# Convolution states of a hybrid encoder layer: one transfer and copies on chip in place of one small transfer for each tile

## The chip, the core and the metric

The kernel runs on one core of a Trainium2 chip. The metric is the device time of one execution in microseconds (us). The engines are TensorE (PE; PEld is its weight load), VectorE (DVE), ScalarE (ACT), GpSimd (POOL) and SyncE (SP), which issues every DMA of this kernel on one queue (SPq in the rows).

## The reference

One step of a one-layer encoder over T = 1152 columns: 1024 of a prompt, then 8 samples of 16. Cut to what matters here:

```
h  = rmsnorm(x);  split(h @ w_in)                # mixer A: sparse attention, mixer B: gated delta rule
ext = concat([conv_b_buf, conv_in])              # 3 old values per channel and sequence, 1536 channels
new_conv_b = ext[:, T:]                          # the last 3 go out as the new state
cb  = silu(causal_dwconv(ext, conv_b))           # width 4, then the delta rule
x   = x + (sigmoid(ga) * ya + sigmoid(gbr) * yb) @ w_out
ext_f = concat([ffn_buf, u_gate])                # 2 old values per channel and sequence, 2816 channels
new_ffn = ext_f[:, T:]
x   = x + (gelu(causal_dwconv(ext_f, conv_ffn)) * u_val) @ w_down
```

The prompt starts from a state of zeros; the 8 samples bring one each (`state_gdn_conv`, `state_ffn_conv`). Both kinds of new state are outputs.

## The kernel before, in words

Channels lie on partitions, time on columns. Products are made of two fp32r parts each (H and L of the activations, wh and wl of the weights), three matmuls for a tile of 128 channels by 384 columns (`acc`), later 288 (`up`) and 384 (`dn`). A small driver in the kernel (`_Driver`) runs many generators as threads against an own clock of costs and writes every engine's instructions in the order that comes out; `yield SP` asks for a place in the DMA queue, `yield self.exts` for a buffer, `yield DMA` or an event for a landing. `pick` gives an element-wise operation to the one of two engines that is free first on that clock. So an edit at one place changes the order of what comes after it on all engines.

The stages, by the time of the profile: normalisation and first products (0 to 120 us); the input projection, with the indexer (`ix`, its queries `qr` loaded from DRAM), the width-4 convolutions of 12 channel tiles, the selection of keys and the local part of the delta rule (`gd`) beside it (120 to 650); attention, the scan of the delta rule and the samples (`at`) with dense products as filler (650 to 1060); the output projection; the `up` products of 22 channel tiles with the width-3 convolution (1205 to 1710); the `down` products (to 2075); the end.

The two places of the change:

- `evac_conv`: an evacuated tile goes into an extended buffer `ext` (two of them, `exts`). In block 2 (last 256 prompt columns and the samples) the view `es` holds 8 rows of 3 + 16 columns. The 3 state columns come by a DMA from `in_sc_b`, 128 partitions by 8 runs of 12 bytes; the last 3 columns of the prompt and of each sample go out by two DMAs to `out_cb`, and `ext` is given back behind them.
- `evac_up` and `up_inner`: the same for the up-projection with a buffer `fe` (two), states of 2 columns: a DMA from `in_sc_f` (8 runs of 8 bytes for each partition), two DMAs to `out_cf`, then `AT[f]` is stored, and `load_up` reads it back (`xs<-AT`) for the down products.

Of the kernel before, what the change touches and what calls it, by code (L numbers as in the profile page):

```python
# [7 lines left out]
F32 = mybir.dt.float32  # L8
# [12 lines left out]
TP = 1024  # L21
# [9 lines left out]
PE, ACT, DVE, POOL, SP, DMA = "pe", "act", "dve", "pool", "sp", "dma"  # L31
# [269 lines left out]
class _Kernel:  # L301
# [382 lines left out]
    def mixers(self):  # L684
        I, drv = self.I, self.drv
# [12 lines left out]
        self.cvp = conv.enter_context(self.tc.tile_pool(name="cv", bufs=1, side="right", reuse_waits="tile"))  # L698
        self.exts = _Banks(self.cvp, [128, 412], "ext", 2)
        self.cvs = _Banks(self.cvp, [128, BW], "cvc", 2)  # L700
        first = [None, 4, 5, 8, 9, 10]
        order = [(f, (0,)) for f in first] + [(None, (1, 2))] + [(f, (0, 1)) for f in range(4)]
        rest = [*range(16, 28), 4, 28, 5, 29, 6, 30, 7, 31, *range(8, 16), *range(32, 48)]
# [61 lines left out]
    def first_loads(self, jobs, p):  # L765

        nc, I, drv = self.nc, self.I, self.drv
# [34 lines left out]
        yield DVE  # L802
        nc.vector.tensor_scalar(self.cwb, self.cwb, 0.5, None, op0=OP.mult)
        nc.vector.tensor_scalar(self.ngd, self.ngd, 0.5, None, op0=OP.mult)

    def arrival(self, ev, t):
        self.drv.cur.dma = t
# [152 lines left out]
    def evac_conv(self, f):  # L960

        nc, O, I = self.nc, self.O, self.I
        h, kind = divmod(f - 16, 4)
        ch = (kind - 1) * 4 + h
        last = self.cvp.tile([128, 2, 3], F32, name="last", bufs=4)

        def go(b, cols, acc):
            w = self.cwb[:, ch]
            ext = yield self.exts
            es = ext[:, 259:411].rearrange("p (b q) -> p b q", q=19)  # L970
            n = BW if b < 2 else 256
            if b < 2:
                yield from self.scaled(ext[:, 3:3 + n], acc, b)
                yield POOL
                nc.gpsimd.tensor_copy(last[:, b], ext[:, BW:BW + 3])
            else:
                yield ACT
                nc.scalar.copy(ext[:, 3:3 + n], acc[:, :n])
                nc.scalar.copy(es[:, :, 3:], acc[:, 256:].rearrange("p (b q) -> p b q", q=16))
                self.drv.give(self.accs, acc)  # L980
            yield POOL
            if b == 0:
                nc.gpsimd.memset(ext[:, 0:3], 0.0)
            else:
                nc.gpsimd.tensor_copy(ext[:, 0:3], last[:, b - 1])
            if b == 2:
                yield SP
                nc.sync.dma_start(es[:, :, 0:3], I["sc_b"][ch])
                yield DMA
            c = yield self.cvs  # L990
            t = yield self.evs
            groups = [(c[:, :n], [ext[:, j:j + n] for j in range(4)])]
# [2 lines left out]
            for o, src in groups:  # L995
                yield ACT
                nc.scalar.activation(o, src[0], AF.Copy, scale=w[:, 0:1])
                for j in range(1, 4):
                    if j == 2:
                        u = t[:, :n] if len(o.shape) == 2 else t[:, 256:].rearrange("p (b q) -> p b q", q=16)  # L1000
                        yield ACT
                        nc.scalar.activation(u, src[j], AF.Copy, scale=w[:, j:j + 1])
                        yield POOL
                        nc.gpsimd.tensor_add(o, o, u)
                    else:
                        yield DVE
                        nc.vector.scalar_tensor_tensor(o, src[j], w[:, j:j + 1], o, op0=OP.mult, op1=OP.add)
            if b == 2:
                yield SP
                nc.sync.dma_start(O["cb"][ch][:, 0:3], ext[:, 256:259])  # L1010
                nc.sync.dma_start(O["cb"][ch][:, 3:27].rearrange("p (b q) -> p b q", q=3), es[:, :, 16:19])
            self.drv.give(self.exts, ext)
            yield ACT
            nc.scalar.activation(t, c, AF.Tanh)
            yield DVE
# [1547 lines left out]
    def evac_out(self, d):  # L2563
# [61 lines left out]
            drv.give(self.xs, x)  # L2625
        return go

    def up_parts(self, t):

        nc = self.nc  # L2630
# [35 lines left out]
    def evac_up(self, j, bank):  # L2666

        nc, drv, p, f = self.nc, self.drv, self.fp, j.f
# [20 lines left out]
        drv.give(self.ups, bank[A1X])  # L2689
        ext = yield self.exts  # L2690
        es = ext[:, 1026:].rearrange("p (b q) -> p b q", q=18)
        yield SP
        nc.sync.dma_start(es[:, :, 0:2], self.I["sc_f"][f])
        yield POOL
        nc.gpsimd.memset(ext[:, 0:2], 0.0)
        g, R = parts(ext[:, 2:2 + T]), parts(self.R2)
        if f == 0:

# [13 lines left out]
            x = own(u1)  # L2712
        else:
# [12 lines left out]
            x = own(u2)  # L2726
# [10 lines left out]
    def up_inner(self, j, ext, v):  # L2737

        nc, drv, f = self.nc, self.drv, j.f
# [4 lines left out]
        for o, src in ((c[:, :512], [ext[:, k:k + 512] for k in range(3)]),  # L2744
# [4 lines left out]
            for k in (1, 2):  # L2749
                yield DVE  # L2750
                nc.vector.scalar_tensor_tensor(o, src[k], cw[:, k:k + 1], o, op0=OP.mult, op1=OP.add)
        yield SP
        nc.sync.dma_start(self.O["cf"][f][:, 0:2], ext[:, TP:TP + 2])
        nc.sync.dma_start(self.O["cf"][f][:, 2:18].rearrange("p (b q) -> p b q", q=2), es[:, :, 16:18])
        drv.give(self.exts, ext)
        yield ACT
        nc.scalar.activation(c, c, AF.Gelu_apprx_tanh)
# [231 lines left out]
    def merge_ffn(self):  # L2989
# [41 lines left out]
        with ExitStack() as st:  # L3031
            self.fp = fp = self.pool(st, "ff")
            self.exts = _Banks(fp, [128, 1026 + 144], "fe", 2)
            self.cs = _Views([])
            self.vs = _Banks(fp, [128, T], "fv", 2)
            self.fev.t = 0.0
            for n, t in enumerate((0, 2, 3)):
                drv.spawn(self.up_parts(t), n)
# [68 lines left out]
def _layout(np, x):  # L3107
# [18 lines left out]
    for n in ("w_proj_a", "w_proj_b", "w_out", "w_up", "w_down", "w_ple", "w_ple_gate"):  # L3126
# [9 lines left out]
    a["cv"] = asc(x["cache_v"][0].reshape(8, 256, 512))  # L3136
    a["ckiT"] = asc(x["cache_kidx"][0].transpose(2, 0, 1))
    a["s0"] = asc(x["state_gdn"][0].transpose(1, 2, 0, 3))
    a["sc_b"] = asc(x["state_gdn_conv"][0].transpose(2, 0, 1).reshape(12, 128, 8, 3))
    a["sc_f"] = asc(x["state_ffn_conv"][0].transpose(2, 0, 1).reshape(22, 128, 8, 2))  # L3140
    return a


_OUTS = {"yT": (1024, T), "kT": (512, T), "vT": (512, T), "kiT": (64, T), "gp": (4, 128, 128),
         "gs": (4, 128, 8, 128), "cb": (12, 128, 27), "cf": (22, 128, 18)}


def _collect(np, r):
    asc = np.ascontiguousarray
    y, k, ki = r["yT"].T, r["kT"].T, r["kiT"].T  # L3150
    v = r["vT"].T
    cb, cf = r["cb"].reshape(1536, 27).T, r["cf"].reshape(2816, 18).T
    out = (y[:TP].reshape(1, TP, 1024), y[TP:].reshape(8, 16, 1024),
           k[:TP].reshape(1, 1, TP, 8, 64), v[:TP].reshape(1, 1, TP, 8, 64), ki[:TP].reshape(1, 1, TP, 64),
           r["gp"].reshape(1, 1, 4, 128, 128), cb[:3].reshape(1, 1, 3, 1536), cf[:2].reshape(1, 1, 2, 2816),
# [21 lines left out]
```

## Time and profile before

| | |
|---|---|
| median of 3 runs | 2109.88 us (2105.96 to 2117.38) |
| the profiled execution | 2107.12 us, span from first to last instruction 2105.0 us |
| busy share of the span | PE 97%, PEld 95%, DVE 73%, ACT 48%, POOL 39% |
| granted TensorE clock, mean | 0.992 |
| DMA | 319403 packets, 314.56 MB, 117532 packets under 512 bytes |

Idle time of an engine counts only where the span's end hangs on it. A line of the profile names an operation by what it writes and reads (`acc<-H,wh`). All operations are recorded by one helper, so that every row names line 192, and tiles tell them apart.

### The profile page before, as it was taken

How to read it: one execution, taken by the hardware profiler on the slowest of the kernel's cores; microseconds unless marked ns; L12 is line 12 of the kernel's file. 1: busy time of each engine (PE TensorE's matmuls, PEld its weight loads, DVE VectorE, ACT ScalarE, POOL GpSimd, SP SyncE). 2: the span in 40 equal slices, each digit the busy share in tenths (PEclk: the TensorE clock that was granted, in tenths of full speed). 3: DMA queues.
4: the chain of work that ended last, by engine and by line, in shares of the span. 5: the costliest groups of instructions: out<-in, count | busy, mean ns of one | idle time of the engine just before them, and what ended most of it. 6: DMA issues, size and time to landing. Idle time of an engine off the chain costs nothing.

```text
span 2105.0 us, 37636 instructions
## 1 busy us (share of the span) xinstructions
PE 2049.5 (97%) x13176; PEld 1998.2 (95%) x13176; DVE 1530.6 (73%) x3578; ACT 1011.0 (48%) x1999; POOL 826.0 (39%) x998
## 2 busy tenths in 40 slices
PE   7999999999999999999999999999999999999998
PEld 6898999999999899999999999999999999999997
DVE  7267989989815777776455888888888766767656
ACT  5266677676324555576333443333333344535433
POOL 5334544432323434554363355556555500210102
PEclk9999999999999999999999999999999999999998
DMA  5444377686448474566674423434444486657543
GB/s 199 112 131 94 90 197 189 165 191 196 137 131 255 146 216 142 156 214 204 196 233 155 142 67 74 83 67 74 76 69 80 91 189 211 195 177 224 174 138 99
DMA packets 319403, 314.56 MB, mean 149 GB/s; under 512 B 117532, under 2 KB 278256, under 8 KB 319088
## 3 DMA queue, kind: packets, MB, share of 16 engines
q1 hardware_dynamic: 319216, 312.17, 54.3%
q8 instruction: 104, 1.70, 0.4%
q14 instruction: 83, 0.68, 0.1%
HBM read 224.91 MB, written 88.81 MB: 149 GB/s over the span
## 4 chain that ended last, share of the span: by engine, by line
PE 81%; DMA 7%; DVE 6%; ACT 2%; issue 2%; SPq 1%; POOL 1%; DVEq 0%; POOLq 0%; ACTq 0%
PE acc L192 30%; PE up L192 23%; PE dn L192 17%; PE at L192 6%; PE gd L192 3%; PE ix L192 1%; SPq L192 1%; DMA obT<-sg 1%; DVE e L192 1%; DMA qr<-qiT 1%; DMA sg<-sgb 1%; DVE z L192 1%; PE ac L192 1%; DMA evo<-gates 1%; DMA xs<-AT 1%
## 5 line engine op out<-in xcount | busy, mean ns | idle before, releaser
L192 PE MATMUL acc<-H,wh 128*128 128x384 f32 (+2 forms) x1344 | 475.4, 354 | 6.2 <-ACT ext L192 3.9
L192 PE MATMUL acc<-L,wh 128*128 128x384 f32 (+2 forms) x1344 | 455.7, 339 | 1.4 <-DVE L L192 1.1
L192 PE MATMUL acc<-H,wl 128*128 128x384 f32 (+2 forms) x1344 | 455.7, 339 | 0.0
L192 POOL TENSOR_TENSOR wl<-wr,wh 128x256 fp32r<-128x256 f32 (+2 forms) x257 | 216.7, 864 | 289.0 <-ACT wh L192 268.1
L192 PEld LDWEIGHTS acc<-H,wh 128*128 128x128 f32 (+1 forms) x1344 | 252.9, 188 | 14.6 <-ACT ext L192 4.8
L192 PEld LDWEIGHTS acc<-L,wh 128*128 128x128 f32 (+1 forms) x1344 | 253.1, 188 | 6.3 <-DVE L L192 2.4
L192 PEld LDWEIGHTS acc<-H,wl 128*128 128x128 f32 (+1 forms) x1344 | 252.2, 188 | 1.2
L192 POOL TENSOR_TENSOR ssq<-ssq,sqs 128x384 f32<-128x384 f32 x61 | 70.8, 1160 | 380.6 <-ACT sqs L192 369.7
L192 ACT CAST wh<-wr 128x1024 fp32r<-128x1024 f32 (+3 forms) x140 | 122.7, 883 | 110.8 <-PE dn L192 30.9
L192 POOL TENSOR_TENSOR wl<-s,wh 128x256 fp32r<-128x256 f32 x102 | 96.8, 967 | 142.2 <-ACT wh L192 139.6
L192 PE MATMUL up<-B,wh 128*128 128x288 f32 x704 | 142.3, 296 | 0.0
L192 DVE SCALAR_TENSOR_TENSOR T<-fe,cwf,T 128x512 f32<-128x512 f32 x132 | 122.0, 924 | 17.3 <-ACT T L192 15.9
L192 PEld LDWEIGHTS up<-B,wh 128*128 128x128 f32 x704 | 112.8, 188 | 0.1
L192 ACT ACTIVATE ja<-SC,cola 128x768 bf16<-128x768 f32 (+2 forms) x93 | 96.6, 1039 | 22.4 <-DVE cola L192 13.7
L192 ACT CAST wh<-s 128x512 fp32r<-128x512 f32 x88 | 52.5, 620 | 111.7 <-PE up L192 102.3
L192 PE MATMUL up<-B,wl 128*128 128x288 f32 x352 | 104.0, 295 | 0.0
L192 PE MATMUL up<-T,wh 128*128 128x288 f32 x352 | 103.5, 294 | 0.0
L192 DVE TENSOR_TENSOR wl<-wr,wh 128x512 fp32r<-128x512 f32 (+1 forms) x95 | 80.2, 858 | 27.6 <-ACT wh L192 27.6
L192 POOL TENSOR_TENSOR cvc<-cvc,evo 128x384 f32<-128x384 f32 (+2 forms) x48 | 44.0, 917 | 89.9 <-ACT evo L192 65.7
L192 ACT ACTIVATE z<-z,mx 128x896 f32<-128x896 f32 (+7 forms) x83 | 63.2, 766 | 19.6 <-DVE mx L192 19.2
L192 DVE TENSOR_SCALAR_CACHE_REDUCE e<-half,colv 128x384 bf16<-128x384 int16 (+5 forms) x96 | 71.0, 739 | 0.7
L192 PEld LDWEIGHTS up<-T,wh 128*128 128x128 f32 x352 | 66.1, 188 | 0.0
(511 smaller groups left out, 6094.2 us busy)
## 6 DMA issues: line engine op xcount, KB each, us to landing
wr<-in_w_in SPq DMA_DIRECT2D x48, 512.0 KB, 3.8
AT<-fv SPq DMA_DIRECT2D x22, 576.0 KB
wr<-in_w_down SPq DMA_DIRECT2D x24, 512.0 KB, 3.7
T<-in_w_down SPq DMA_DIRECT2D x24, 512.0 KB, 4.1
wr<-in_w_up SPq DMA_DIRECT2D x22, 512.0 KB, 4.2
gates<-evo SPq DMA_DIRECT2D x48, 192.0 KB, 4.7
T<-AT SPq DMA_DIRECT2D x44, 192.0 KB, 4.5
qkv<-evo SPq DMA_DIRECT2D x36, 192.0 KB, 5.2
```

The lines of the kernel that those rows point to most:

```text
L192: r = f(*a, **k)
```

## The change

Both states come in one DMA each and stay on chip: `scb` (128 x 12 x 8 x 3), loaded behind the constants, and `scf`, which takes one of the two `sqs` buffers for the whole up stage. POOL copies a tile's part into `ext` or `fe`. The new states are copied into `cbs` by ACT and into `cfs` by POOL; `cbs` goes out once, `cfs` after tile 10 and after tile 21. The layouts of these four arrays in DRAM are turned on the host so that a partition's part is one run. `ext` is given back as soon as the taps are issued.

```diff
@@ mixers
+        self.scb = self.cvp.tile([128, 12, 8, 3], F32, name="scb")
+        self.cbs = self.cvp.tile([128, 12, 9, 3], F32, name="cbs")
+        self.scev, self.cbn = _Event(), 0
@@ first_loads
+        yield self.fin[4][0]
+        yield SP
+        nc.sync.dma_start(self.scb, I["sc_b"])
+        yield DMA
+        drv.set(self.scev)
@@ evac_conv
+            if b == 2:
+                yield self.scev
             yield POOL
...
             if b == 2:
-                yield SP
-                nc.sync.dma_start(es[:, :, 0:3], I["sc_b"][ch])
-                yield DMA
+                nc.gpsimd.tensor_copy(es[:, :, 0:3], self.scb[:, ch])
+                yield ACT
+                nc.scalar.copy(self.cbs[:, ch], ext[:, 240:411].rearrange("p (b q) -> p b q", q=19)[:, :, 16:19])
...
+            self.drv.give(self.exts, ext)
             if b == 2:
-                yield SP
-                nc.sync.dma_start(O["cb"][ch][:, 0:3], ext[:, 256:259])
-                nc.sync.dma_start(O["cb"][ch][:, 3:27].rearrange("p (b q) -> p b q", q=3), es[:, :, 16:19])
-            self.drv.give(self.exts, ext)
+                self.cbn += 1
+                if self.cbn == 12:
+                    yield SP
+                    nc.sync.dma_start(O["cb"], self.cbs)
@@ up_states (new)
+        s = yield self.sqs
+        self.scf = s[:, :352].rearrange("p (f b q) -> p f b q", b=8, q=2)
+        yield SP
+        self.nc.sync.dma_start(self.scf, self.I["sc_f"])
+        yield DMA
+        self.drv.set(self.sfev)
+        for e in self.uev:
+            yield e
+        self.drv.give(self.sqs, s)
@@ evac_up
-        yield SP
-        nc.sync.dma_start(es[:, :, 0:2], self.I["sc_f"][f])
+        yield self.sfev
         yield POOL
         nc.gpsimd.memset(ext[:, 0:2], 0.0)
+        nc.gpsimd.tensor_copy(es[:, :, 0:2], self.scf[:, f])
@@ up_inner
-        yield SP
-        nc.sync.dma_start(self.O["cf"][f][:, 0:2], ext[:, TP:TP + 2])
-        nc.sync.dma_start(self.O["cf"][f][:, 2:18].rearrange("p (b q) -> p b q", q=2), es[:, :, 16:18])
+        yield POOL
+        nc.gpsimd.tensor_copy(self.cfs[:, f % 11], ext[:, 1008:1170].rearrange("p (b q) -> p b q", q=18)[:, :, 16:18])
+        if f % 11 == 10:
+            yield SP
+            nc.sync.dma_start(self.O["cf"][f // 11], self.cfs)
         drv.give(self.exts, ext)
```

What it does to the order of the instructions, at three places. First the DMA queue (SP) in the convolution stage, around the second convolution tile's last block; `qr` are the indexer's queries, `wr` a weight tile, `qkv` a finished convolution tile going out. Before:

```order
110 L192 DMA qkv<-evo_1663 128x384
111 L192 DMA selE<-in_selE 128x240
112 L192 DMA qr<-qiT 64x384 x2
113 L192 DMA kb<-in_ckiT 64x256 x2
114 L192 DMA out_cb<-ext_1611 128x3
115 L192 DMA out_cb<-ext_1611 128x8x3
116 L192 DMA wr<-in_w_in 128x1024
117 L192 DMA qkv<-evo_1694 128x384
118 L192 DMA qr<-qiT 64x384 x2
119 L192 DMA ext_1853<-in_sc_b 128x8x3
```

and now:

```order
109 L192 DMA selE<-in_selE 128x240
110 L192 DMA qr<-qiT 64x384 x2
111 L192 DMA kb<-in_ckiT 64x256 x2
112 L192 DMA wr<-in_w_in 128x1024
113 L192 DMA qr<-qiT 64x384 x2
114 L192 DMA qkv<-evo_1748 128x384
115 L192 DMA sgb<-evo_1815 128x384
116 L192 DMA qr<-qiT 64x384 x2
```

The two stores of states and the load of states are gone, and the next queries stand directly behind the weight tile.

Second the same queue where the up products end and the down products begin; `T` and `wr` are raw down weights, `xs` the columns of `AT` that are read back, `B` columns of the residual. Before:

```order
1047 L192 DMA xs_19676<-AT 128x384
1048 L192 DMA xs_19697<-AT 128x384
1049 L192 DMA out_cf<-fe_19289 128x2
1050 L192 DMA out_cf<-fe_19289 128x8x2
1051 L192 DMA T_19719<-in_w_down 128x1024 x2
1052 L192 DMA xs_19723<-AT 128x384
1053 L192 DMA xs_19730<-AT 128x384
1054 L192 DMA xs_19760<-AT 128x384
1055 L192 DMA xs_19765<-AT 128x384
1056 L192 DMA B_19770<-x2T 128x384
```

and now:

```order
955 L192 DMA xs_19643<-AT 128x384
956 L192 DMA xs_19649<-AT 128x384
957 L192 DMA xs_19685<-AT 128x384
958 L192 DMA T_19694<-in_w_down 128x1024 x2
959 L192 DMA xs_19692<-AT 128x384
960 L192 DMA xs_19703<-AT 128x384
961 L192 DMA xs_19728<-AT 128x384
962 L192 DMA B_19741<-x2T 128x384
```

The state of tile 20 no longer stands ahead of the two weight loads; one more load of `AT` does.

Third POOL in the up stage, one tile's stretch; `s` are sums of raw up weights, `wl` their low parts. Before:

```order
698 L192 MEMSET fe_18809 128x2
699 L192 TENSOR_TENSOR wl<-s_18594,wh 128x256 x2
700 L192 TENSOR_TENSOR s_18872<-wv 128x512
701 L192 TENSOR_TENSOR s_18891<-s_18872,wg 128x512
702 L192 TENSOR_TENSOR s_18909<-wg,wv 128x512
703 L192 TENSOR_TENSOR wl<-s_18685,wh 128x256 x2
704 L192 TENSOR_TENSOR s_18956<-s_18891,wg 128x512
```

and now:

```order
712 L192 MEMSET fe_18781 128x2
713 L192 COPY fe_18781<-sqs_14369 128x8x2
714 L192 TENSOR_TENSOR wl<-s_18571,wh 128x256 x2
715 L192 TENSOR_TENSOR s_18844<-wv 128x512
716 L192 TENSOR_TENSOR s_18863<-s_18844,wg 128x512
717 L192 TENSOR_TENSOR s_18881<-wg,wv 128x512
718 L192 TENSOR_TENSOR wl<-s_18661,wh 128x256
719 L192 COPY cfs<-fe_18543 128x18
720 L192 TENSOR_TENSOR wl<-s_18661,wh 128x256
721 L192 TENSOR_TENSOR s_18927<-s_18863,wg 128x512
```

Two copies per tile have come in among the weight operations, one behind the memset and one for the tile before.

## Rows read from the trace of the kernel before

**Rows 1.** Busy time by engine in stretches: us, then PE, PEld, DVE, ACT, POOL.

```profile
120.00:460.00 340.00, 329.21 (x1897) 316.46 (x1896) 303.16 (x898) 241.34 (x498) 148.39 (x221) 0.98 0.61 150
460.00:650.00 190.00, 189.41 (x1251) 181.15 (x1250) 118.11 (x374) 82.25 (x168) 55.46 (x72) 1.00 0.60 171
650.00:1060.00 410.00, 394.55 (x2654) 377.21 (x2653) 283.84 (x927) 232.77 (x578) 178.46 (x265) 1.00 0.63 188
1240.00:1700.00 460.00, 460.00 (x3470) 460.00 (x3470) 379.52 (x500) 158.46 (x260) 256.07 (x251) 1.00 0.40 77
1700.00:1730.00 30.00, 27.43 (x154) 26.37 (x153) 19.98 (x38) 13.37 (x19) 0.00 (x0) 1.00 1.02 236
...
sum 2105.00, PE 2049.46 PEld 1998.19 DVE 1530.61 ACT 1010.97 POOL 826.04; mean PE 204.95 PEld 199.82 DVE 153.06 ACT 101.10 POOL 82.60
```

**Rows 2.** Issues by tile on the page: count, KB each, median us to landing.

```profile
x2T<-xs SPq DMA_DIRECT2D x24, 192.0 KB, 2.1
...
fe<-in_sc_f SPq DMA_DIRECT2D x22, 8.0 KB, 3.0
...
out_cf<-fe SPq DMA_DIRECT2D x22, 8.0 KB, 8.5
...
out_cb<-ext SPq DMA_DIRECT2D x12, 12.0 KB, 6.8
```

**Rows 3.** Stretches of two us in the convolution stage, columns as in rows 1.

```profile
174.00:176.00 2.00, 2.00 (x13) 1.92 (x12) 2.00 (x7) 1.57 (x4) 0.00 (x0) 1.00 0.68 68
...
180.00:182.00 2.00, 0.00 (x0) 0.00 (x0) 0.58 (x2) 1.16 (x2) 0.00 (x0) 1.00 0.53 155
```

**Rows 4.** The chain that ended last, the piece there: start, us, what.

```profile
172.50 8.27 DMA qr<-qiT
```

**Rows 5.** Waits from 120 to 460 us: total, times, longest.

```profile
ACT ext L192 <- DMA out_cb<-ext: 5.1, 4, 2.4
...
PE acc L192 <- ACT ext L192: 3.9, 3, 2.6
...
PE ix L192 <- DVE qs L192: 2.1, 1, 2.1
```

**Rows 6.** Stretches where up ends and down begins, columns as in rows 1.

```profile
1704.00:1706.00 2.00, 2.00 (x13) 2.00 (x13) 0.31 (x3) 0.00 (x0) 0.00 (x0) 1.00 1.31 41
...
1708.00:1710.00 2.00, 1.11 (x7) 0.79 (x5) 0.00 (x0) 0.43 (x1) 0.00 (x0) 1.00 0.97 377
1710.00:1712.00 2.00, 1.23 (x5) 0.91 (x6) 1.35 (x3) 1.87 (x4) 0.00 (x0) 1.00 1.07 391
...
1722.00:1724.00 2.00, 1.68 (x10) 1.27 (x8) 2.00 (x6) 2.00 (x4) 0.00 (x0) 1.00 1.44 307
1724.00:1726.00 2.00, 1.40 (x8) 1.40 (x9) 2.00 (x5) 1.02 (x2) 0.00 (x0) 1.00 1.24 66
```

**Rows 7.** Timeline there, DMA queue and ACT: start, us, what, idle before.

```profile
1695.94 2.04 SPq L192 DMA_DIRECT2D out_cf<-fe  x2
1698.03 1.05 SPq L192 DMA_DIRECT2D T<-in_w_down  x2
...
1709.57 1.04 ACT L192 CAST T3H<-T 128x1024 fp32r<-128x1024 f32 x1 [7.90 <-DMA T<-in_w_down]
```

**Rows 8.** The DMA queue's own waits from 1240 to 1700 us.

```profile
SPq L192 <- DMA out_cf<-fe: 35.6, 10, 8.0
```

**Rows 9.** Operations like the added ones: ns min/median/max; the moved ones: us, mean ns.

```profile
L192 POOL COPY last<-ext x24: 183/202/1174, 122.1 to 411.1; 128x3 f32<-128x3 f32 x24
...
L192 DVE TENSOR_TENSOR wl<-s,wh 128x512 fp32r<-128x512 f32 x31 | 28.2, 911 | 13.3 <-ACT wh L192 13.2
L192 DVE TENSOR_TENSOR s<-wr 128x512 f32<-128x512 f32 x9 | 9.6, 1066 | 0.3
```

**Rows 10.** A stretch with a hole and what the clock did (PEclk stands behind POOL).

```profile
275.00:300.00 25.00, 21.71 (x116) 20.95 (x116) 24.05 (x86) 17.54 (x38) 10.54 (x20) 0.93 0.89 213
```

**Rows 11.** The chain that ended last, a stretch of dense products alone: start, us, what.

```profile
1057.67 145.72 PE acc L192 x834
```

More of the change, by code (lines that the diff above doesn't have):

```diff
@@ L2626, in evac_out, with up_states @@
         return go
+    def up_states(self):
+        s = yield self.sqs
[7 more added lines that the diff above has]
+        self.drv.give(self.sqs, s)
     def up_parts(self, t):
@@ L3035, in merge_ffn @@
             self.vs = _Banks(fp, [128, T], "fv", 2)
+            self.cfs = fp.tile([128, 11, 9, 2], F32, name="cfs", bufs=1)
+            self.sfev = _Event()
+            drv.spawn(self.up_states(), 2)
             self.fev.t = 0.0
@@ L3138, in _layout @@
     a["s0"] = asc(x["state_gdn"][0].transpose(1, 2, 0, 3))
-    a["sc_b"] = asc(x["state_gdn_conv"][0].transpose(2, 0, 1).reshape(12, 128, 8, 3))
-    a["sc_f"] = asc(x["state_ffn_conv"][0].transpose(2, 0, 1).reshape(22, 128, 8, 2))
+    a["sc_b"] = asc(x["state_gdn_conv"][0].transpose(2, 0, 1).reshape(12, 128, 8, 3).transpose(1, 0, 2, 3))
+    a["sc_f"] = asc(x["state_ffn_conv"][0].transpose(2, 0, 1).reshape(22, 128, 8, 2).transpose(1, 0, 2, 3))
     return a
 _OUTS = {"yT": (1024, T), "kT": (512, T), "vT": (512, T), "kiT": (64, T), "gp": (4, 128, 128),
-         "gs": (4, 128, 8, 128), "cb": (12, 128, 27), "cf": (22, 128, 18)}
+         "gs": (4, 128, 8, 128), "cb": (128, 12, 9, 3), "cf": (2, 128, 11, 9, 2)}
 def _collect(np, r):
@@ L3151, in _collect @@
     v = r["vT"].T
-    cb, cf = r["cb"].reshape(1536, 27).T, r["cf"].reshape(2816, 18).T
+    cb = r["cb"].transpose(2, 3, 1, 0).reshape(27, 1536)
+    cf = r["cf"].transpose(3, 4, 0, 2, 1).reshape(18, 2816)
     out = (y[:TP].reshape(1, TP, 1024), y[TP:].reshape(8, 16, 1024),
```

## The prediction

> **What bounds the kernel now.** I read the stretches first, because an average over this kernel hides its stages. TensorE is busy 2049.5 of 2105.0 us [rows 1], so all its holes together are 55.5 us, and whatever the change does to other engines, it can be paid out only in holes of PE or in its clock. The two halves of the change lie in different stages. The up stage from 1240 to 1700 has no hole at all: 460.00 of 460.00. Its DMA queue does wait, 35.6 us in ten waits for the stores of states [rows 8], but nothing on PE comes from that. From 120 to 460, where the width-4 convolutions are, PE has holes of 10.8 us and a mean clock of 0.98. At the turn from up to down, 1700 to 1730, the holes are 2.6 us. The stretch from 650 to 1060 has 15.5, and the change doesn't edit anything there, though it moves it [all rows 1]. So what can be won directly is 13.4 us of holes and a little clock, 0.6% of the run.
>
> Next I looked at what ends those holes. The reader should see two things. A store of 8 KB lands after 8.5 us and one of 12 KB after 6.8, while 192 KB in long runs take 2.1 [rows 2]; it is the number of runs (128 x 8 of 8 or 12 bytes) and not the bytes. And while such a store is under way the DMA engines are busy without moving data: 0.68 busy at 68 GB/s at 174 us [rows 3], 1.31 at 41 GB/s at 1704 [rows 6]. What was issued behind it is late. The clearest cases are a `qr` load of 8.27 us in the chain that ended last, from 172.50 [rows 4], then PE empty from 180 to 182 [rows 3], and the two down weights that were issued at 1698.03 right behind a store at 1695.94 and that ACT could take only at 1709.57, after 7.90 us of idling [rows 7].
>
> **The change part by part.** *Removed.* 12 loads and 24 stores in the convolution stage, 22 loads and 44 stores in the up stage; five DMAs replace these 102. The slow stores cost 12 x (6.8 - 2.1) + 22 x (8.5 - 2.1) = 197 us of a DMA path that is otherwise free for the loads behind them [rows 2]. Almost all of that lies beside PE work. What shows on PE is three things:
>
> (a) The indexer's stall. PE waited 2.1 us for the split queries [rows 5] and the stretch 180 to 182 is empty [rows 3]. Without the store the load should come about 6.8 - 2.1 = 4.7 us sooner, more than the hole: -2.1. Bounds 0 (the 512 KB weight tile now directly ahead of it in the order takes the place) and -2.1.
>
> (b) The extended buffer. ACT waited four times, 5.1 us in all, for `out_cb` to give `ext` back, and PE three times, 3.9 us, for ACT's evacuation into `ext` [rows 5]. `ext` is now free after the taps. The rows don't pair the waits; ACT has 98.7 us idle in this stage [rows 1], so a late copy need not be due to the store. I take one of the three, 1.3 us. Bounds 0 and -3.9.
>
> (c) The turn. The holes at 1708 to 1712 are 0.89 + 0.77 and those at 1722 to 1726 0.32 + 0.60 [rows 6]. The first two wait for a weight that the store held up by more than their length. The last two come from the same queue, which then catches up at 307 to 391 GB/s. -2.6; bounds 0 and -2.6. In the up stage before it, the freed DMA queue gives nothing, as PE covers all of it; if that cover were gone, the 35.6 us of waits would be the most there is [rows 8].
>
> *Clock.* The 25 us around a 3.3 us hole at 290 ran at 0.93 [rows 10], which is 25 x 0.07 = 1.8 us. That hole is not plainly one of those above, so I take 0, with -1.8 as its bound.
>
> *Added.* 12 copies of `scb`, 22 of `scf`, 22 into `cfs` on POOL, 12 into `cbs` on ACT. The nearest row is POOL's copy of three columns, 0.20 us in the median and 0.18 to 1.17 between the ends [rows 9]. POOL has 204 us idle in the up stage and 192 in the convolution stage [rows 1]; 44 x 0.20 = 9 us and 12 x 0.20 = 2.4 us go into that. At 1.17 us each, 51 and 14 us, they still fit. Behind such a copy stand low parts of weights (`wl`), and PE waits for those only when the buffers run out, which the full stretch from 1240 excludes so far. Value 0. ACT's 12 copies are 2.4 us by the same row, in 98.7 us of idling: 0. The first `scf` copy waits for its load, issued at the place where the first `fe` load stood, with 3.0 us to land [rows 2] and 8.5 as the worst; behind it on POOL is one sum of squares. 0, worst 1. The wait of the driver for `scb` is over long before block 2 of the first tile.
>
> One page bears against the copies. The Trainium skill, "SBUF — State Buffer", section "SBUF: two separate sides", says that VectorE and GpSimd share one pair of ports, held by one of them for a whole instruction while the other stands still. The trace agrees as far as it goes: the same copy takes 0.18 or 1.17 us [rows 9]. By the rule each copy could also stop DVE for 0.2 us, 2.4 us in the convolution stage, and the sum would be 2103.5 in place of 2101.1.
>
> *Moved.* The driver's clock now runs differently, and `pick` puts work elsewhere: counted in the two orders, 18 pieces of `wl` on POOL become 9 on DVE, 9 sums `s` go from POOL to DVE, and 10 scalings in the attention go from ACT to DVE. In the up stage that is 9 x 0.91 + 9 x 1.07 = 17.8 us more DVE [rows 9], 379.5 + 17.8 = 397 of 460 [rows 1]: hidden; it would cost only beyond the 80.5 us that are free. The order of PE from 460 on changes too; its price is not in the trace. Between nothing and the second rival's price below, I take 0, since the work is the same and only its mixing differs.
>
> **Sum.** 2107.1 - 2.1 - 1.3 - 2.6 = 2101.1 against the profiled execution (span 2105.0 and 2.1 around it). The median of the three runs is 2109.9, 2.8 above that execution, within a spread of 11 us; against the median the sum would be 2103.9. I give 2102.5.
>
> **Rivals.** *First, the convolution stage fills up.* Shorter DMA times help every chain there and not only the two waits that I priced. All 10.8 us of holes go, with half of the clock's 0.02 x 340 = 6.8, and the 2.6 at the turn: -16.8, 2090. For it: 56 of the 197 us of slow stores fall in this stage. Against it: DVE is busy 303 of 340 us there [rows 1], so some holes wait for DVE whatever the DMA does.
>
> *Second, slower.* The attention chain comes later in PE's order. Counted in the orders, 2694 dense matmuls stand ahead of the first `at` matmul before and 2727 now, and ahead of the 600th 3114 and 3198. A dense matmul is 145.72 / 834 = 0.175 us [rows 11], so the chain starts 5.8 us and at the 600th is 14.7 us later behind PE work. Where this chain, and not the sum of PE's work, sets the end of the stretch 650 to 1060, that comes on top: 2106.9 to 2115.8, say 2111. For it: PE has holes in that stretch although dense filler stands ready [rows 1]. Against it: 15.5 in 410 us is little, so PE's work sets most of it. It decides when the holes there grow by more than the 6.0 us won, to over 21.5.
>
> *Third, nothing.* The loads behind the stores were also behind weight tiles of 512 KB, and waits only change their name: 2107 to 2110.
>
> *Fourth, the port rule above*: 2103.5, which would not tell itself from the forecast by time.
>
> **How the numbers follow.** Forecast 0.48, first rival 0.22, second 0.17, third 0.10, fourth 0.03. A change below about 0.5%, 10.5 us, can't be told from none here. Beyond it on the fast side lie the first rival and the forecast's end with every bound taken (2.1 + 3.9 + 2.6 + 1.8 = 10.4): 0.26. On the slow side only the upper end of the second with more holes than it prices: 0.09. The rest, 0.65, is no change that could be told. The forecast's own range is 2097 to 2107, from all bounds to none. With both first rivals in, 2091 to 2113.
>
> **What would show it.** Packets under 512 bytes fall from 117532 to some 44 thousand (102 DMAs hold about 74 thousand runs). (a) no wait of PE `ix` for `qs` of 2 us, and `qr` loads of about 2 to 5 us; (b) no line of ACT or POOL that waits for `out_cb`; (c) less than 1 us of holes in the 30 us after the last up product, and ACT's `T3H` cast within 5 us of the load; (d) no hole in the up stage, with POOL copies of about 0.2 us. I am wrong if the stretch of attention and samples has over 21 us of holes, if holes appear in the up stage, or if the convolution stage keeps its 10.8 us under other names.

## The result and the profile after

The changed kernel takes 2098.8 us in the median of ten runs (2091.5 to 2104.0), the kernel before on the same chip 2111.2 (2106.0 to 2117.4): a ratio of 0.994 with a 95% interval of 0.9925 to 0.9955. That is 12.4 us, a little beyond the half per cent that can be told from no change. The profiled execution took 2099.05 us (span 2097.2), 8.1 less than that of before; the forecast's sum had 6.0 less.

The same stretches of the changed kernel, columns as in [rows 1]:

```profile
120.00:460.00 340.00, 332.70 (x1937) 321.81 (x1936) 304.34 (x893) 226.24 (x481) 154.74 (x242) 0.99 0.53 160
460.00:650.00 190.00, 190.00 (x1258) 181.80 (x1257) 120.84 (x377) 100.37 (x199) 50.19 (x66) 1.00 0.55 162
650.00:1060.00 410.00, 397.55 (x2678) 381.38 (x2677) 297.71 (x952) 225.76 (x575) 185.00 (x271) 1.00 0.64 191
...
1205.00:1240.00 35.00, 32.67 (x228) 32.43 (x227) 21.30 (x39) 10.71 (x19) 17.00 (x17) 0.90 0.15 46
1240.00:1700.00 460.00, 460.00 (x3462) 459.70 (x3461) 385.75 (x525) 159.31 (x261) 242.23 (x263) 1.00 0.25 81
1700.00:1730.00 30.00, 30.00 (x173) 30.00 (x172) 18.73 (x35) 13.21 (x20) 0.47 (x1) 1.00 0.74 256
```

Against [rows 1], the convolution stage has 7.3 us of holes in place of 10.8, the turn from up to down none in place of 2.6, and the up stage from 1240 is as full as it was. New is the stretch from 1205 to 1240, where the up stage begins: 2.3 us of holes and a clock of 0.90. The page gives the packets; most of the small ones are gone, as forecast (some 44 thousand under 512 bytes):

```profile
DMA packets 244506, 314.54 MB, mean 150 GB/s; under 512 B 41996, under 2 KB 203360, under 8 KB 244192
```

The added copies on POOL, grouped by form (count, then us in all and mean ns of one, then idle time before them):

```profile
L192 POOL COPY fe<-sqs 128x16 f32<-128x16 f32 x22 | 12.4, 562 | 5.2 <-DMA sqs<-in_sc_f 5.2
...
L192 POOL COPY cfs<-fe 128x18 f32<-128x18 f32 x22 | 5.8, 261 | 13.4 <-DVE fe L192 13.4
...
L192 POOL COPY ext<-scb 128x24 f32<-128x24 f32 x12 | 2.8, 234 | 0.0
```

Fixed windows compare different work once one kernel is ahead. So I cut each profiled execution at three instructions: the first indexer product (`ix`), the first `up` product and the first `dn` product; the last piece ends with the start of the last `rp` product. These are the rows of the changed kernel for two of the cuts (ns min/median/max, then first and last start in us):

```profile
L192 PE MATMUL up<-B1H,wh x176: 293/296/377, 1196.2 to 1676.6; 128*128 128x288 f32 x176
```
```profile
L192 PE MATMUL dn<-B1H,wh x96: 333/338/424, 1696.1 to 2015.9; 128*128 128x384 f32 x96
```

All executions cut in this way, in us, with the ratio to before that each kernel measured on its own chip (the experiments are told below):

| kernel | first ix to first up | up stage | first dn to last rp | median, ratio (95%) |
|---|---|---|---|---|
| before | 1096.1 | 494.5 | 395.3 | 2111.2, 1 |
| changed | 1084.0 | 499.9 | 392.0 | 2098.8, 0.994 (0.9925 to 0.9955) |
| changed, again | 1080.5 | 498.6 | 392.0 | 2097.1, 0.9942 (0.9921 to 0.9963) |
| before, long stores | 1086.5 | 494.5 | 393.3 | 2097.5, 0.9963 (0.9946 to 0.998) |
| changed, small stores | 1117.0 | 496.9 | 399.0 | 2136.1, 1.0141 (1.0119 to 1.0163) |
| convolution half | 1085.8 | 494.4 | 393.7 | 2095.3, 0.9945 (0.9927 to 0.9964) |
| convolution half, again | 1088.4 | 494.5 | 394.9 | 2096.4, 0.9935 (0.9916 to 0.9955) |
| up half | 1092.9 | 498.6 | 392.0 | 2107.8, 1.0003 (0.9988 to 1.0017) |
| convolution load only | 1099.6 | 494.5 | 394.0 | 2113.1, 1.0038 (1.0023 to 1.0052) |
| order for quick stores | 1109.2 | 494.5 | 395.2 | 2121.4, 1.0074 (1.0054 to 1.0094) |
| first load direct | 1085.0 | 494.6 | 392.0 | 2092.5, 0.994 (0.992 to 0.996) |
| first load direct, again | 1085.5 | 494.6 | 396.0 | 2094.0, 0.9936 (0.9916 to 0.9955) |
| no single up load | 1086.1 | 494.5 | 392.3 | 2093.6, 0.9944 (0.9924 to 0.9965) |
| copy put back | 1081.2 | 494.7 | 391.0 | 2093.6, 0.9952 (0.9936 to 0.9969) |

The up half has the order of before up to the up stage, so its 3.2 us in the first column show how far two executions of the same work lie apart there. Between the two executions of the changed kernel it is 3.5. Ahead of the first `ix`, which the table leaves out, the changed execution took 112.2 us and that of before 109.9; the four executions without `scb` have one order of instructions up to there and lie between 109.9 and 112.1, so that this 2.4 us is not told from chance.

The reader is to see three things in the table. Some 12 us are won between the first `ix` and the first `up`, where the sum had 3.4 (the kernels with quick convolution stores win 7.7 to 15.6 there). Some 3 are won after it, where the sum had 2.6. And 4 to 5 are lost in the up stage, where the sum had nothing.

### The profile page after: what moved, and what is told of

The parts are those of the page before. It is cut to its first block, busy times and chain, and to the rows that moved or that the text cites. A ratio compares the mean times of both kernels' runs of the same rounds, so it can differ in the third digit from the quotient of the medians.

```text
span 2097.2 us, 37414 instructions
## 1 busy us (share of the span) xinstructions
PE 2049.6 (98%) x13176; PEld 2002.2 (95%) x13176; DVE 1542.4 (74%) x3606; ACT 1002.7 (48%) x2002; POOL 817.4 (39%) x1026
## 4 chain that ended last, share of the span: by engine, by line
PE 85%; DMA 5%; DVE 4%; ACT 1%; issue 1%; POOL 1%; SPq 1%; POOLq 0%; DVEq 0%; ACTq 0%
PE acc L192 33%; PE up L192 23%; PE dn L192 18%; PE at L192 6%; PE gd L192 3%; PE ix L192 1%; SPq L192 1%; DMA sg<-sgb 1%; DMA obT<-sg 1%; PE rp L192 1%; DVE z L192 1%; PE ac L192 1%; DMA kL<-kTs 1%; POOL ssq L192 0%; DMA xb<-in_xT 0%
## 5 line engine op out<-in xcount | busy, mean ns | idle before, releaser
L192 POOL TENSOR_TENSOR wl<-s,wh 128x256 fp32r<-128x256 f32 x84 | 78.2, 949 | 130.3 <-ACT wh L192 130.3
L192 DVE SCALAR_TENSOR_TENSOR T<-fe,cwf,T 128x512 f32<-128x512 f32 x132 | 114.3, 866 | 15.2 <-ACT T L192 14.2
L192 PEld LDWEIGHTS up<-B,wh 128*128 128x128 f32 x704 | 114.0, 190 | 0.0
L192 DVE TENSOR_TENSOR wl<-T,wh 128x512 fp32r<-128x512 f32 x64 | 45.2, 730 | 32.8 <-ACT wh L192 32.8
L192 ACT ACTIVATE evo<-acc 128x384 f32<-128x384 f32 x64 | 31.2, 488 | 76.7 <-PE acc L192 71.6
```

What stands on the lines that cost most here:

```text
L192: r = f(*a, **k)
```

## The experiments

Two theories stand against each other for the gain. *Small runs*: the slow stores held up loads and buffers, and without them those come earlier. *Order*: the driver's clock, with other costs, put the work in a better order. A third question came from the trace: what costs 5 us at the start of the up stage.

**Before, long stores.** The order of all instructions on PE, DVE, ACT and POOL is that of before, since the driver is given the old cost (`held`); the stores alone have long runs, and write whole rows of `ext`.

```diff
-                nc.sync.dma_start(O["cb"][ch][:, 3:27].rearrange("p (b q) -> p b q", q=3), es[:, :, 16:19])
+                nc.sync.held = 2.61
+                nc.sync.dma_start(O["cb"][ch][:, 3:155], ext[:, 259:411])
+                nc.sync.held = None
...
-        nc.sync.dma_start(self.O["cf"][f][:, 2:18].rearrange("p (b q) -> p b q", q=2), es[:, :, 16:18])
+        nc.sync.held = 2.61
+        nc.sync.dma_start(self.O["cf"][f][:, 2:146], ext[:, 1026:1170])
+        nc.sync.held = None
```

> The kernel before with every instruction of PE, DVE, ACT and POOL in its old order; only the 34 stores of 8 and 12 byte pieces are one run of 576 or 608 bytes per partition (they write whole rows, and the state is cut out of them after the run). Theory 'small runs' (the change won because the slow stores held up loads and buffers): terms (a) to (c) of the prediction appear without any reordering, -6.0 us and up to -10.4 with every bound, ratio 0.995 to 0.997; the store of the convolution stage lands in about 2 to 3 us in place of 6.8, that of the up stage in 2 to 3 in place of 8.5, no ACT wait for out_cb, no PE wait of 2.1 us for qs, and the holes at 1700 to 1730 fall from 2.6 to under 1. Theory 'order' (the change won because the driver's clock put the work in another order): 0 to -3 us, ratio 0.9985 to 1.000, with the holes of 120 to 460 still near 10.

Measured: ratio 0.9963 (0.9946 to 0.998), so with nothing reordered the stores win 4 to 11 us. The DMA issues from 120 to 460 and from 1240 to 1740 us, with KB each and the median us to landing:

```profile
qr<-qiT SPq DMA_DIRECT2D x27, 96.0 KB, 3.5
...
out_cb<-ext SPq DMA_DIRECT2D x12, 76.0 KB, 2.5
```
```profile
out_cf<-fe SPq DMA_DIRECT2D x21, 72.0 KB, 3.2
```

Six and nine times the bytes of [rows 2] land in 2.5 and 3.2 us in place of 6.8 and 8.5, and the `qr` loads of 96 KB around them in 3.5 us, where the execution before shows 7.0:

```profile
qr<-qiT SPq DMA_DIRECT2D x26, 96.0 KB, 7.0
```

Where the holes went is seen in three stretches of 20 us, columns as in [rows 1], first of before, then with long stores, then of the changed kernel:

```profile
180.00:200.00 20.00, 17.91 (x96) 16.87 (x97) 16.67 (x29) 14.31 (x23) 7.55 (x9) 1.00 0.42 86
280.00:300.00 20.00, 16.71 (x88) 16.03 (x87) 19.57 (x77) 13.08 (x28) 7.27 (x14) 0.91 1.00 229
340.00:360.00 20.00, 17.77 (x103) 17.27 (x102) 19.86 (x62) 15.01 (x32) 11.40 (x19) 1.00 0.98 234
```
```profile
180.00:200.00 20.00, 20.00 (x110) 18.86 (x109) 17.36 (x30) 15.13 (x26) 7.88 (x11) 1.00 0.33 96
280.00:300.00 20.00, 16.92 (x91) 16.20 (x91) 19.12 (x77) 12.22 (x26) 6.14 (x13) 0.91 1.02 306
340.00:360.00 20.00, 20.00 (x118) 19.86 (x117) 19.96 (x79) 14.31 (x32) 8.98 (x16) 1.00 0.86 254
```
```profile
180.00:200.00 20.00, 20.00 (x111) 18.72 (x109) 18.28 (x29) 14.25 (x23) 7.22 (x8) 1.00 0.35 103
280.00:300.00 20.00, 20.00 (x118) 19.92 (x117) 15.03 (x46) 12.90 (x28) 12.59 (x21) 1.00 0.72 232
340.00:360.00 20.00, 18.69 (x109) 17.99 (x108) 20.00 (x81) 15.74 (x37) 8.51 (x15) 1.00 0.71 212
```

The indexer's hole at 180 goes with the stores. The hole at 350 goes too; the sum did not have it. There PE waited for a load `vc<-qkv`, before:

```profile
350.41 0.63 PE L192 MATMUL gd<-c,vc 128*128 128x128 f32 x4 [2.23 <-DMA vc<-qkv]
```

The DMA queue held that load back until an earlier store out of a `vc` buffer, `gsc<-vc`, had landed, as the profile puts it; that store stands just ahead of `out_cb`. The queue of before (start, us, what), its waits for that store (total, times, longest), and then the queue with long stores:

```profile
339.09 0.37 SPq L192 DMA_DIRECT2D gsc<-vc  x1
339.51 1.71 SPq L192 DMA_DIRECT2D out_cb<-ext  x2
...
345.39 0.33 SPq L192 DMA_DIRECT2D vc<-qkv  x1
```
```profile
SPq L192 <- DMA gsc<-vc: 4.6, 3, 2.9
```
```profile
336.31 0.37 SPq L192 DMA_DIRECT2D gsc<-vc  x1
336.73 1.74 SPq L192 DMA_DIRECT2D out_cb<-ext  x2
...
339.80 0.32 SPq L192 DMA_DIRECT2D vc<-qkv  x1
```

The load is issued 6.3 us after `gsc<-vc` in the one and 3.5 in the other; of that the queue waited 2.9 and 0.2 us for the store. So here a store in small runs also held up a transfer that was issued 0.4 us ahead of it. The hole at 290 stays, though ACT no longer waits for `out_cb` anywhere: PE's waits for `ext` are the 3.9 us of [rows 5] almost unchanged.

```profile
PE acc L192 <- ACT ext L192: 3.7, 3, 2.6
```

The longest of them ends with this copy, which on ACT stands behind operations of the selection (`ja`) that leave ACT no idle time (ACT, then PE):

```profile
288.90 1.15 ACT L192 ACTIVATE ja<-SC,cola 128x1024 bf16<-128x1024 f32 x1
...
290.46 0.53 ACT L192 COPY ext<-acc 128x256 f32<-128x256 f32 x2
```
```profile
291.04 0.44 PE L192 MATMUL acc<-H,wh 128*128 128x384 f32 x1 [2.56 <-ACT ext L192]
```

**Changed, small stores.** The order is the changed kernel's; the small stores are put back beside its own, unseen by the driver, to outputs that nobody reads.

```diff
+            if b == 2:
+                sync = nc.sync.eng
+                sync.dma_start(O["cbx"][ch][:, 0:3], ext[:, 256:259])
+                sync.dma_start(O["cbx"][ch][:, 3:27].rearrange("p (b q) -> p b q", q=3), es[:, :, 16:19])
             self.drv.give(self.exts, ext)
...
+        sync = nc.sync.eng
+        sync.dma_start(self.O["cfx"][f][:, 0:2], ext[:, TP:TP + 2])
+        sync.dma_start(self.O["cfx"][f][:, 2:18].rearrange("p (b q) -> p b q", q=2), es[:, :, 16:18])
```

> The changed kernel with the 68 small stores of before put back beside its own (to extra outputs), unseen by the driver: PE, DVE, ACT and POOL keep the order of the changed kernel. Theory 'small runs': the 12.4 us go back by 6 to 10 us, to about 2105 to 2109; the holes of 1700 to 1730 and a wait for a small store in the convolution stage come back. Theory 'order': at most 3 us slower than the changed kernel, 2099 to 2102.

Measured: 1.4% slower than before, so more than any theory had: the stores cost some 8 us in the old order (0.0037 of 2107), and some 42 in the new one (1.0141 less 0.994, of 2107). Its convolution stage and the wait behind it:

```profile
120.00:460.00 340.00, 312.37 (x1735) 300.08 (x1734) 275.56 (x773) 208.55 (x443) 139.58 (x225) 0.96 0.55 143
```
```profile
ACT ext L192 <- DMA out_cbx<-ext: 29.3, 6, 14.7
...
PE acc L192 <- ACT ext L192: 12.8, 1, 12.8
```

The changed order takes the next `ext` at once, because it counts on having it back after the taps. With a store that still reads `ext`, ACT stands for up to 14.7 us.

**One half each.** The diffs are the two halves of the change's own; what is not named stays as before.

> The convolution half of the change alone (the up stage as before). By the terms of the prediction -2.1 - 1.3 = -3.4 us, ratio 0.998, with the holes at the turn from up to down still 2 to 3 us. By the stages of the two traces, where PE's last indexer product came 7 us earlier and the turn gave some 3.5 more: -8 us or more, ratio 0.996, and no loss of some 5 us at the start of the up stage, so that it could stand at 2098 to 2102.

> The up half of the change alone (the convolution stage as before). By the prediction -2.6 us, all of it at the turn from up to down, ratio 0.999. By the trace of the changed kernel the wait of POOL for the one state load in front of a sum of squares costs a hole of 2.3 us and some 3.2 us of a lower clock at the start of the up stage, which eats the gain of the turn: +1 to +3 us, ratio 1.000 to 1.0015. Whichever: instructions up to 1190 us in the same order as before, with holes of 10 to 11 us in 120 to 460.

Measured: 0.9945 and 1.0003; the first, at 2095.3 us, gained some 3 us more than the stages of the two traces had let me expect. The whole gain is in the convolution half. The up half wins 3.3 us at the turn and loses 4.1 in the up stage (table), so that nothing is left. Between the two theories: long stores in the old order give 0.9963, the convolution half and the whole change, in a new order, 0.9935 to 0.9945. The intervals overlap, so small runs are shown to be a cause, and what the new order adds to quick stores is not shown by the times.

**Convolution load only, and order for quick stores.** In the first, states come in one load with POOL's copies, and the stores stay as before (its diff is a part of the change's own). In the second, the program's transfers are those of before, but the driver thinks the stores quick.

```diff
+                nc.sync.held = 0.1
                 nc.sync.dma_start(O["cb"][ch][:, 3:27].rearrange("p (b q) -> p b q", q=3), es[:, :, 16:19])
+                nc.sync.held = None
...
```

> Of the convolution half only its load: the states come in one transfer and are copied by POOL, the 24 small stores and all of the up stage are as before. Theory 'small stores': the loads of 2.5 us were hidden, and the stores keep their cost: within 4 us of before, ratio 0.998 to 1.002. Rival 'loads matter': half or more of the 11.8 us that the convolution half won alone, ratio 0.997 or less.

> The kernel before with its small transfers, but the driver is told that the long one of each pair of state stores takes 0.1 us of the queue in place of 2.61, so that it orders the work as if the stores were quick. Theory 'small runs': the order alone gains nothing, and an order that counts on quick stores is paid for when they are slow (the changed order with the small stores was 29 us slower than before, for other reasons too): 2107 to 2120, ratio 1.000 to 1.006. Theory 'order': 2095 to 2102, ratio 0.994 to 0.998.

Measured: 1.0038 and 1.0074, both slower than before, and both beyond what any of the theories gave (at most 1.002 and 1.006). The single load wins nothing by itself; but it came with another order too, so the load alone was not measured. Of the 6.1 us by which its profiled span is longer (2111.1), 3.5 lie between the first `ix` and the first `up` in the table, and 4.0 ahead of the first `ix`, where the one load, issued at 35 us, is the only difference. Executions with that load take between 110.2 and 114.0 us to the first `ix`, those without it 109.9 to 112.1, so a price of the load there is not told from chance; which operation the 3.5 come from stays open. The order for quick stores loses 15.9 us while the stores are slow, and much of what it waits for is what small runs make late (waits from 120 to 460; 5.1 us in [rows 5]). It is an order of its own, and not that of the changed kernel:

```profile
ACT ext L192 <- DMA out_cb<-ext: 15.2, 4, 5.2
```

**The start of the up stage.** In the changed kernel POOL's first copy waits 5.21 us for the one load, and the sum of squares `ssq` behind it takes 5.61 us, for which PE waits and after which its clock falls to half. POOL, then PE, then VectorE (start, us, what, idle before):

```profile
1201.57 0.43 POOL L192 COPY fe<-sqs 128x16 f32<-128x16 f32 x1 [5.21 <-DMA sqs<-in_sc_f]
1201.99 5.61 POOL L192 TENSOR_TENSOR ssq<-ssq,sqs 128x384 f32<-128x384 f32 x1
```
```profile
1207.66 1.44 PE L192 MATMUL rp<-ones,ssq 128*128 128x1 f32 x6 [2.33 <-POOL ssq L192]
```
```profile
1202.19 0.69 DVE L192 TENSOR_TENSOR s<-s,wr 128x512 f32<-128x512 f32 x1
1202.79 1.42 DVE L192 TENSOR_TENSOR T<-T,T2H 128x576 fp32r<-128x576 f32 x2
1204.12 0.69 DVE L192 TENSOR_TENSOR wl<-s,wh 128x512 fp32r<-128x512 f32 x1
...
1206.00 0.76 DVE L192 TENSOR_TENSOR T<-T,T2H 128x576 fp32r<-128x576 f32 x1
```

Behind PE's wait, the granted clock is at its lower level, 1.2 of 2.4 GHz, for these 6 us (us, PE busy, clock, then DMA share and GB/s):

```profile
1208.00:1214.00 6.00, 6.00 (x27) 0.50 0.00 0
```

So 2.3 us of hole and 3.0 us of clock make nearly all of the 5.4 us of the table. The kernel with small stores put back has the same hole (`ssq` stood for 5.62 us there) with the clock at 1.00, and its up stage is 2.4 us longer than that of before. My first theory was that the late load is the cause. Two kernels avoid it: one loads the first tile's states directly, the other has no single load in the up stage at all.

```diff
-        yield self.sfev
+        if f == 0:
+            yield SP
+            nc.sync.dma_start(es[:, :, 0:2], self.I["sc_f"][:, 0])
+        else:
+            yield self.sfev
         yield POOL
         nc.gpsimd.memset(ext[:, 0:2], 0.0)
-        nc.gpsimd.tensor_copy(es[:, :, 0:2], self.scf[:, f])
+        if f:
+            nc.gpsimd.tensor_copy(es[:, :, 0:2], self.scf[:, f])
```

> The changed kernel, but the states of the first up tile are loaded straight into its buffer in 8 byte pieces, as before, so that POOL's first copy does not wait for the one load of 176 KB with a sum of squares behind it. Theory 'late load': the up stage, first `up` product to first `dn` product, takes 494 to 496 us as in the kernel before (499.9 in the changed one), no PE wait of 2 us for `ssq`, clock 1.00 in the 35 us around the start: 4 to 5 us less than the changed kernel, 2093 to 2096, ratio 0.992 to 0.9935. Rival 'held by VectorE': that sum of squares took 5.61 us in place of 1.03 because VectorE worked beside it without a pause, and will do so again whether or not POOL waited before: the wait of PE for it stays at 1 to 2 us, and 0 to 2 us are won.

> The changed kernel without the one load of the up stage's states (each tile loads its own again, in 8 byte pieces); its two stores in long runs stay. Theory 'late load': as for the run above, the up stage takes 494 to 496 us, and as the turn keeps its gain of 3 us: 2092 to 2096, ratio 0.992 to 0.9935, no slower than the run above, since the loads of 3 us were never waited for. Rival 'loads cost too': the 22 loads stand ahead of weights and the turn from up to down has 1 us or more of holes again, 2096 to 2099.

Measured: the up stage takes 494.6 and 494.5 us, as the theory 'late load' said; the ratios are 0.994 and 0.9944, a little above its 0.9935. As the kernel before differed from chip to chip by several us, three kernels ran once more on one chip.

> The changed kernel itself, on the same chip as the two runs beside it, since the kernel before stood between 2105.6 and 2111.2 us from chip to chip. Theory 'late load': its up stage is 4 to 5 us longer than that of the kernel with the first tile's states loaded directly, so it is 3 to 6 us slower than that one, ratio to before 0.993 to 0.997. Rival 'noise': the 5 us at the start of the up stage were those of one execution, and the two agree within 2 us.

> The changed kernel with the first up tile's states loaded directly, again. Theory 'late load': 3 to 6 us faster than the changed kernel on this chip, ratio to before 0.991 to 0.9945, up stage 494 to 495 us. Rival 'noise': within 2 us of the changed kernel.

> The convolution half alone, again. If the two halves add, it is slower than the run with the direct first load by what the turn from up to down gains, 1.5 to 3 us, and faster than the changed kernel by the loss at the start of the up stage less that gain, 1 to 3 us. If the up half is worth nothing at all once its loss is mended, it agrees with the run with the direct first load within 1 us.

Measured: 2097.1, 2094.0 and 2096.4 us, with intervals that overlap almost wholly: a difference of 3 us between these three is not shown by their times. The up stage is: 498.6, 494.6 and 494.5. And the second execution of the changed kernel spoke against the late load. There it is the copy that stands, for 4.82 us, and `ssq` is quick:

```profile
1191.84 0.10 POOL L192 MEMSET fe<- 128x2 f32 x1 [1.70 <-PE acc L192]
1197.57 4.82 POOL L192 COPY fe<-sqs 128x16 f32<-128x16 f32 x1 [5.63 <-DMA sqs<-in_sc_f]
1202.34 0.99 POOL L192 TENSOR_TENSOR ssq<-ssq,sqs 128x384 f32<-128x384 f32 x1
```

POOL gets going 5.6 us after its memset in the kernels without the loss too, since `ssq` has to wait that long for ACT (5.63 us in the kernel with the direct load). What differs is how long it then takes.

```profile
1201.61 2.42 POOL L192 TENSOR_TENSOR ssq<-ssq,sqs 128x384 f32<-128x384 f32 x1 [5.63 <-ACT sqs L192]
```

So the last kernel puts the copy, with its wait, back on POOL into the faster order, unseen by the driver (against the kernel with the direct load).

```diff
-        if f:
-            nc.gpsimd.tensor_copy(es[:, :, 0:2], self.scf[:, f])
+        q = nc.gpsimd if f else nc.gpsimd.eng
+        q.tensor_copy(es[:, :, 0:2], self.scf[:, f])
```

> The kernel with the first up tile's states loaded directly, and POOL's first copy out of the one load put back unseen by the driver (it writes the same values a second time): the order of PE, DVE, ACT and SP is that of the faster kernel, POOL's has the copy, with its wait for the load, ahead of the sum of squares. In the three executions with the loss that sum of squares was ready to start at the same 5.6 us after the memset as in the executions without it, and then it or the copy stood for about 5 us beside back-to-back two-input operations of VectorE. Theory 'order of VectorE': the loss hangs on VectorE having two operations on `T` in a row there, without a gap that lets POOL in; with the other order the copy comes and goes: up stage 494 to 495 us, the copy and the sum of squares together under 4 us, no PE wait of 2 us for `ssq`. Theory 'late load': the copy's wait brings the loss back, up stage 498 to 500 us.

Measured: up stage 494.7 us. The copy waits even longer (part of it for the tile's own load, which it overwrites), and nothing is lost. POOL, then VectorE:

```profile
1201.39 0.65 POOL L2725 COPY fe<-sqs 128x16 f32<-128x16 f32 x1 [6.59 <-DMA fe<-in_sc_f]
1202.00 1.02 POOL L192 TENSOR_TENSOR ssq<-ssq,sqs 128x384 f32<-128x384 f32 x1
```
```profile
1201.23 0.75 DVE L192 TENSOR_TENSOR T<-T,T2H 128x576 fp32r<-128x576 f32 x1
1202.01 1.56 DVE L192 TENSOR_TENSOR wl<-s,wh 128x512 fp32r<-128x512 f32 x1
1203.49 1.86 DVE L192 TENSOR_TENSOR T<-T,T2H 128x576 fp32r<-128x576 f32 x1
```

The late load has fallen: POOL starts as late as in the kernels with the loss, and the up stage is as short as before. In the slower order VectorE has two `T<-T,T2H` in a row and then runs without a gap to 1206.8 (the first three rows shown overlap by 0.09 us where they join); POOL stands until then. In the faster order `wl` comes after one of them, a gap of 0.03 us lies ahead of it (1201.23 + 0.75 to 1202.01), POOL gets in, and now VectorE's operations take 1.56 and 1.86 us in place of 0.69 and 0.76. All four executions with the slower order (the changed kernel twice, the up half, the small stores put back) have a POOL operation that stands for 4.8 to 5.6 us, and in the ten with the faster order none there takes more than 2.43. No run keeps the slower order and takes POOL's copy away, so the order of VectorE as the cause is what all the rows fit, and not a test of its own. What makes the gap is not in the rows.

## Why the prediction came out as it did

The range and the direction held; the time lay 3.7 us under the figure given, and the mechanism of slow stores is shown (long stores in an unchanged order: 0.9963). That the time lies in the range is in part luck. The gain of 12.4 us is twice the sum's 6.0 and more than all its bounds together, 10.4; the range hung on 2107 us for before, which over ten runs stands at 2111.2, and a loss that the sum did not have took 4 to 5 us of the gain away; without it the time would lie at some 2094, under the range. The steps, one by one:

(a) *The indexer's stall*, -2.1: right. The hole at 180 us goes with the stores alone, by 2.09 us, and `qr` loads have a median of 3.5 us or less.

(b) *The extended buffer*, -1.3: this step failed. The wait of ACT for `out_cb` is what small runs cause, and it goes with them, but the PE waits that I tied to it stay (3.7 of 3.9 us in the unchanged order). ACT was late there by its own queue. In the changed kernel, whose order is another, these waits are gone, and so are the 3.3 us of holes at 280 to 300 and with them the clock of 0.91 there, which is 20 x 0.09 = 1.8 us. That is most of the bound of -3.9 and all of that of -1.8, by another cause than I gave; which part of the new order does it, no run tells apart. The remark that a late copy need not be due to the store was right.

*Missing*: PE's wait of 2.23 us for `vc` at 350, two steps from a slow store. I looked for tiles that the store touches and the loads directly behind it, not for a transfer ahead of it that lands late too, and a load that waits for that one. With the stores alone made long, (a) and this wait make 4.3 of the 4.8 us by which the holes from 120 to 460 shrink (10.8 to 340 - 334.01 = 6.0). The changed order has other holes from 300 on, two waits for `vc` of 2.1 us in all among them, and keeps 7.3.

(c) *The turn*, -2.6: right. In the 40 us from the first `dn` product PE has holes of 1.6 to 3.5 us in all six executions with small up stores, 2.6 of them in that of before, and of at most 0.15 us in all eight without. The whole piece to the end is less clear: 391.0 to 393.3 us in seven of the eight, 393.7 to 399.0 with small up stores, but 396.0 in the second execution with the direct load, which lost its time later.

*Added copies*, 0 with a worst case of 1: this term was mis-sized. It costs 4.1 to 5.4 us in the change and its up half, at one place. The copies themselves are close enough (0.23 to 0.56 us against 0.20) and hidden. I had priced the wait for the load, and that is hidden, as my 0 had it; the price is that an operation of POOL stood for 5 us beside VectorE.

*Moved work*, 0: my reason, that the same work only mixes differently, did not hold. With quick stores the new order is worth little that the times can show, though it fills the hole at 290; with slow stores two other orders cost 0.7 and 1.4% (1.0074, and 1.0141 for the changed kernel's own); and at the start of the up stage the new order of VectorE is the one with the loss.

The rivals: the convolution stage did not fill up (7.3 us of holes are left). The later attention chain did not show, with 12.5 us of holes from 650 to 1060 against 15.5. The port rule gave a cost, not where I looked (VectorE stopped by the convolution's copies) but where a POOL operation stood for VectorE.

So the changed kernel's execution stands against its sum as follows: between the first `ix` and the first `up` 12.1 us won in place of 3.4, in the up stage 5.4 lost in place of 0, behind it 3.3 won in place of 2.6, and ahead of the first `ix` 2.4 lost that may be chance. Of the 12.1, fewer holes of PE make 6.9 (3.5 of them from 120 to 460 us, 3.0 from 650 to 1060, where nothing was edited); the rest, 5.2, is clock and what two executions differ by, and I can't tell these apart. The errors of the two sides partly cancelled.

## What to carry to other kernels

A store of a thousand pieces of 8 bytes costs its queue more than one of nine times the bytes in long runs: batch it, or store whole rows and cut on the host, before anything is reordered. What it delays can stand ahead of it on the queue (`gsc<-vc` here) as well as behind. Where a planner sets the order, its idea of a transfer's cost and the transfer itself have to change together, since orders that count on quick stores were 0.7 to 1.4% slower than before with slow ones. And before a loss is put down to the wait that stands ahead of it, put the wait back into the faster order: here POOL was as late again and the loss did not come.

## What the runs showed that I had not expected

A copy of 16 columns on POOL stood for 4.82 us, and a sum that takes 1.03 in the median (2.42 at this place without the loss) stood for 5.61, while VectorE ran seven operations with two tiles as inputs back to back. The copy ended at 1202.39 us, VectorE's last of the seven, in the same execution, at 1202.33:

```profile
1201.57 0.76 DVE L192 TENSOR_TENSOR T<-T,T2H 128x576 fp32r<-128x576 f32 x1
```

The Trainium skill, "SBUF — State Buffer", section "SBUF: two separate sides", says that one of the two engines holds a shared pair of ports for a whole instruction. The trace agrees as far as times can show it, and adds that here it was not one instruction but a row of them, and that POOL got in where VectorE left a gap of 0.03 us (0.01 to 0.03 in the ten executions without the loss).

The runs of a store count more than I had read out of the times to landing: with 76 KB in place of 12 per store, the loads around them landed in half the time (7.0 to 3.5 us).
